# The state space scan of a hybrid encoder: rotation, scan and turn back worked in place in PSUM

## The chip, the cores and the metric

The kernel runs on one core of a Trainium2 chip. Its engines are named as the profile names them: PE (matrix products, with PEld for its weight loads), DVE (vector), ACT (scalar), POOL, and SP, which only issues DMAs here. The metric is the device time of one execution, in microseconds (us), the median over runs. Each engine has its own in-order queue of instructions; an instruction may first wait for semaphores that other engines, or earlier instructions, raise.

## The reference

A trunk of two layers on 256 tokens of width 1024. Layer 0 mixes tokens by a bidirectional diagonal complex state space (S5), layer 1 by dilated window attention; each layer then attends to 256 memory tokens and ends in a squared-ReLU MLP. Only the state space part is touched by the change:

```python
def s5_direction(u, lam_re, lam_im, log_dt, b_re, b_im, c_re, c_im, reverse):
    """u: (B,S,G,16) float32 -> Re(C x_t): (B,S,G,16)."""
    ...
    abar_re = mag * jnp.cos(ang)
    abar_im = mag * jnp.sin(ang)
    ...
    bu_re = jnp.einsum('bsgc,gpc->bsgp', u, bbar_re)
    bu_im = jnp.einsum('bsgc,gpc->bsgp', u, bbar_im)
    ...
    _, _, xr, xi = lax.associative_scan(combine, (a_re, a_im, bu_re, bu_im),
                                        reverse=reverse, axis=1)
    return jnp.einsum('bsgp,gcp->bsgc', xr, c_re) - jnp.einsum('bsgp,gcp->bsgc', xi, c_im)
```

There are 64 groups of 16 channels, 64 complex states per group and two directions. The state follows x(t) = A x(t-1) + B u(t) with a complex diagonal A; the result goes through a gelu and a gated product (GLU).

## The kernel before

**What stands where.** The state space part runs first, then the products that make keys and values of the memory tokens, then GLU, memory attention and MLP of layer 0, then layer 1. The memory's keys and values need nothing from the state space part, so their float32 products (`gemm32`, line 241) are mixed into PE's queue between the state space products, as fill. A framework's scheduler, which works with its own estimates, puts the instructions of the whole program into each engine's queue in advance; program order gives the priorities. On the chip that order is fixed.

**The state space part** (`s5`) works through eight chunks of eight groups each (here a chunk is always such a set of groups; tokens are taken four at a time, which gives 64 positions). A tile of a chunk is 128 rows (direction and state) by 8 groups x 64 positions = 512 numbers, which in float32 is just one PSUM bank. The steps per chunk:

- input weights (`s5_weigh_in`, lines 1029 to 1031): six products and sums on DVE, all operands in SBUF, give V; PE transposes V (line 1036) and ACT copies it from PSUM to VT (line 1038).
- `turn` (lines 749 to 752 on POOL): six products and sums make the rotation table T, two tiles (real, imaginary); T exists twice, so the table of a chunk waits until the scan two chunks earlier has read its own.
- `drive` (line 1075): 32 small products on PE put the chunk's inputs, real and imaginary, into two PSUM banks.
- `scan` (below), on DVE: rotates the inputs into a frame in which A is real (complex product with T), runs a linear recurrence along the positions (`tensor_tensor_scan`, line 1093, with the magnitudes R, which ACT writes at lines 1085 and 1086), and turns the result back (complex product with conjugate T, lines 1097 to 1099). ACT then copies the result xt into X (lines 1102 and 1103).
- `weigh_out` on POOL (lines 1113 to 1115): six products and sums, the output weights W; they are kept for three chunks.
- `impulse` (lines 1130 and 1135): products on PE for the response within four tokens, through DRAM into a small matrix M.
- `read` (lines 1156, 1158): PE reads the states out with X, W and M; gelu on ACT, four transposes on PE (line 1164), a copy on ACT (line 1167), a subtraction on DVE (line 1168), which makes the input of GLU.

The loop calls, for each chunk `ch`: the input weights, turn and drive of `ch + 1`, the scan of `ch`, its impulse response, the read of `ch - 1` and the output weights of `ch + 1`. The scheduler runs the input weights one chunk further ahead, so DVE's queue alternates: scan of `ch`, input weights of `ch + 2`, scan of `ch + 1`.

**PSUM** has eight banks. In this part three hold sums of the memory products and five (`psb`) serve all the rest in turn: transposes of the input weights (two per chunk), the drive's two banks, impulse (one), read and its transposes (two). Before the change a drive's two banks are last read by the fifth DVE instruction of the scan; everything behind works in SBUF tiles: `tmp` (two buffers), z and xt.

## Time and profile before

| What | Value |
| --- | --- |
| Median of 3 runs | 1143.39 us (1140.92 to 1145.66) |
| The profiled execution, its span | 1146.1 us |
| Busy PE / DVE / ACT / POOL, whole span | 1055.5 / 761.0 / 576.5 / 240.5 us |
| Mean granted PE clock | 0.940 |
| State space loop (97.4 to 213.5 us): PE / DVE / POOL busy | 96.42 / 113.29 / 88.83 of 116.10 us, clock 0.76 |

The profile shows one execution; the page states no time for it but its span, from the first to the last instruction. Busy time is that of an engine's own instructions, so an engine that is busy all the time may still be held up inside an instruction, and one that is idle costs nothing unless others wait for it. Rows of the timeline give the start, the length and the instruction, in square brackets the idle time before it and what ended it; each float32 product of PE stands there as two records. Groups by line give shortest, median and longest length in ns.

### The profile page before, as it was taken

How to read it: one execution, taken by the hardware profiler on the slowest of the kernel's cores; microseconds unless marked ns; L12 is line 12 of the kernel's file. 1: busy time of each engine (PE TensorE's matmuls, PEld its weight loads, DVE VectorE, ACT ScalarE, POOL GpSimd, SP SyncE). 2: the span in 40 equal slices, each digit the busy share in tenths (PEclk: the TensorE clock that was granted, in tenths of full speed). 3: DMA queues.
4: the chain of work that ended last, by engine and by line, in shares of the span. 5: the costliest groups of instructions: out<-in, count | busy, mean ns of one | idle time of the engine just before them, and what ended most of it. 6: DMA issues, size and time to landing. Idle time of an engine off the chain costs nothing. (4 is left out here: it accounts for less than half of the span.)

```text
span 1146.1 us, 16845 instructions
## 1 busy us (share of the span) xinstructions
PE 1055.5 (92%) x6526; PEld 866.0 (76%) x6526; DVE 761.0 (66%) x1103; ACT 576.5 (50%) x1024; POOL 240.5 (21%) x186
## 2 busy tenths in 40 slices
PE   4787789899999966999998999999999999999998
PEld 3444455556879856899986887887878988998997
DVE  7999999933768633544456676777864776545444
ACT  6253332336757534444444565576753655545443
POOL 3978877400200001100104003000010000111000
PEclk8788677699999987999998999999999999999999
DMA  8312112235554346565655555545433425555653
GB/s 176 93 50 78 62 32 65 70 100 169 187 170 140 116 101 143 189 199 189 189 180 183 168 175 159 177 154 168 148 113 107 155 103 166 184 186 181 196 190 111
DMA packets 99768, 164.02 MB, mean 143 GB/s; under 512 B 16701, under 2 KB 28551, under 8 KB 99560
## 3 DMA queue, kind: packets, MB, share of 16 engines
q1 hardware_dynamic: 88612, 157.15, 43.6%
q10 hardware_dynamic: 11076, 5.80, 2.7%
q8 instruction: 51, 0.84, 0.3%
q14 instruction: 29, 0.24, 0.1%
HBM read 159.11 MB, written 3.82 MB: 142 GB/s over the span
## 5 line engine op out<-in xcount | busy, mean ns | idle before, releaser
L155 DVE TENSOR_TENSOR wlo<-raw,whi 128x1024 fp32r<-128x1024 f32 x264 | 330.6, 1254 | 254.3 <-ACT whi L154 252.7
L154 ACT CAST whi<-raw 128x1024 fp32r<-128x1024 f32 x264 | 276.5, 1049 | 241.0 <-PE psa L202 137.3
L200 PE MATMUL psa<-whi,xs 128*128 128x512 f32 x448 | 179.2, 400 | 0.7 <-ACT sg L1198 0.7
L201 PE MATMUL psa<-wlo,xs 128*128 128x512 f32 x448 | 178.2, 398 | 0.0
L202 PE MATMUL psa<-whi,xs 128*128 128x512 f32 x448 | 177.8, 397 | 0.0
L272 PE MATMUL psb<-xs,whi 128*128 128x256 f32 x512 | 146.1, 286 | 19.7 <-ACT whi L154 19.7
L285 POOL TENSOR_TENSOR sq<-rl 128x512 f32<-128x512 f32 x32 | 40.0, 1251 | 543.6 <-ACT rl L284 543.6
L276 PE MATMUL psb<-xs,wlo 128*128 128x256 f32 x512 | 145.6, 285 | 0.8 <-DVE wlo L155 0.8
L274 PE MATMUL psb<-xs,whi 128*128 128x256 f32 x512 | 145.6, 285 | 0.0
L272 PEld LDWEIGHTS psb<-xs,whi 128*128 128x128 f32 x512 | 99.1, 194 | 20.8 <-ACT whi L154 19.9
L241 PE MATMUL psa<-raw,mT 128*128 128x512 f32 x192 | 103.9, 690 | 0.3 <-DMA raw<-in_xattn_w_kv 0.3
L201 PE MATMUL psa<-wlo,hh 128*128 128x512 f32 x256 | 99.8, 390 | 0.0
L200 PE MATMUL psa<-whi,hh 128*128 128x512 f32 x256 | 99.8, 390 | 0.0
L202 PE MATMUL psa<-whi,hl 128*128 128x512 f32 x256 | 99.7, 389 | 0.0
L276 PEld LDWEIGHTS psb<-xs,wlo 128*128 128x128 f32 x512 | 98.9, 193 | 1.0 <-DVE wlo L155 1.0
L274 PEld LDWEIGHTS psb<-xs,whi 128*128 128x128 f32 x512 | 99.1, 193 | 0.5
L200 PEld LDWEIGHTS psa<-whi,xs 128*128 128x128 f32 x448 | 85.2, 190 | 17.4 <-ACT sg L1198 1.2
L202 PEld LDWEIGHTS psa<-whi,xs 128*128 128x128 f32 x448 | 85.2, 190 | 16.7
L201 PEld LDWEIGHTS psa<-wlo,xs 128*128 128x128 f32 x448 | 85.1, 190 | 16.7 <-DVE wlo L155 0.9
L241 PEld LDWEIGHTS psa<-raw,mT 128*128 128x128 f32 x192 | 40.6, 224 | 43.4 <-issue 41.6
L202 PEld LDWEIGHTS psa<-whi,hl 128*128 128x128 f32 x256 | 48.1, 188 | 10.0
L200 PEld LDWEIGHTS psa<-whi,hh 128*128 128x128 f32 x256 | 48.1, 188 | 9.7
(326 smaller groups left out, 1703.0 us busy)
## 6 DMA issues: line engine op xcount, KB each, us to landing
raw<-in_mlp_w SPq DMA_DIRECT2D x128, 512.0 KB, 3.9
raw<-in_attn_w_qkv SPq DMA_DIRECT2D x72, 512.0 KB, 3.7
raw<-in_xattn_w_kv SPq DMA_DIRECT2D x32, 512.0 KB, 4.1
raw<-in_s_w_glu SPq DMA_DIRECT2D x16, 512.0 KB, 3.8
raw<-in_xattn_w_q SPq DMA_DIRECT2D x16, 512.0 KB, 3.4
raw<-in_xattn_w_o SPq DMA_DIRECT2D x16, 512.0 KB, 4.0
raw<-in_attn_w_o SPq DMA_DIRECT2D x8, 512.0 KB, 3.4
bias_d<-f ACTq DMA_DIRECT2D x1, 1536.0 KB
```

Of the source, the lines that this page charges most:

```text
L154: self.nc.scalar.copy(hi, src)
L155: self.nc.vector.tensor_sub(lo, src, hi.bitcast(F32))
L200: nc.tensor.matmul(acc[t], xh[:, k0 + k, sl], hi[:, k % 2, :], start=st, stop=False)
L201: nc.tensor.matmul(acc[t], xh[:, k0 + k, sl], lo[:, k % 2, :], start=False, stop=False)
L202: nc.tensor.matmul(acc[t], xl[:, k0 + k, sl], hi[:, k % 2, :], start=False, stop=en)
L241: nc.tensor.matmul(acc[t], xT[:, k + q, t * P:(t + 1) * P], raw[:, q, :], start=k + q == 0, stop=k + q == KT - 1)
L272: nc.tensor.matmul(o, hi[:, k % 2, fs], xh[:, kt, :], start=st, stop=False, skip_group_check=True)
L274: nc.tensor.matmul(o, hi[:, k % 2, fs], xl[:, kt, :], start=False, stop=False, skip_group_check=True)
L276: nc.tensor.matmul(o, lo[:, k % 2, fs], xh[:, kt, :], start=False, stop=en, skip_group_check=True)
L285: nc.gpsimd.tensor_mul(sq, rl, rl)
```

## The change

The complex products and the recurrence of `scan` no longer go through SBUF tiles. The two products with the real input go to two SBUF scratch tiles; the two with the imaginary input overwrite the two banks; sum and difference, the recurrence and, in the same order, the turn back work in place in the banks. Only the last sum and difference leave PSUM, into xt. The tile z is gone. Each DVE instruction of the scan has one input in PSUM and one in SBUF. The arithmetic is the same, with the same number of instructions. All other hunks remove only comments, and move line numbers behind the scan by 8.

```diff
         def scan(ch):
...
             nc.scalar.mul(R[:, :, 0:1], R[:, :, 0:1], 0.0)
-            z = ph.tile([P, 2, 8, 64], F32, tag="z", name="z")
             tm = lambda: self.tmp(early, 8, 64)
-            self.cmul(v, [z[:, 0], z[:, 1]], Ss.pop(ch), [T[:, 0], T[:, 1]], tm)
+            S0, S1 = Ss.pop(ch)
+            p, q = tm(), tm()
+            v.tensor_tensor(p, S0, T[:, 0], op=ALU.mult)
+            v.tensor_tensor(q, S0, T[:, 1], op=ALU.mult)
+            v.tensor_tensor(S0, S1, T[:, 1], op=ALU.mult)
+            v.tensor_tensor(S1, S1, T[:, 0], op=ALU.mult)
+            v.tensor_tensor(S0, p, S0, op=ALU.subtract)
+            v.tensor_tensor(S1, S1, q, op=ALU.add)
             rf = R.rearrange("p g k -> p (g k)")
-            for ri in range(2):
-                zf = z[:, ri].rearrange("p g k -> p (g k)")
+            for z in (S0, S1):
+                zf = z.rearrange("p g k -> p (g k)")
                 v.tensor_tensor_scan(zf, rf, zf, 0.0, op0=ALU.mult, op1=ALU.add)
             xt = ph.tile([P, 2, 8, 64], F32, tag="xt", name="xt")
-            for o, (p0, p1, op) in enumerate(((0, 1, ALU.add), (1, 0, ALU.subtract))):
-                t0, t1 = tm(), tm()
-                v.tensor_tensor(t0, T[:, p0], z[:, 0], op=ALU.mult)
-                v.tensor_tensor(t1, T[:, p1], z[:, 1], op=ALU.mult)
-                v.tensor_tensor(xt[:, o], t0, t1, op=op)
+            p, q = tm(), tm()
+            v.tensor_tensor(p, S0, T[:, 0], op=ALU.mult)
+            v.tensor_tensor(q, S0, T[:, 1], op=ALU.mult)
+            v.tensor_tensor(S0, S1, T[:, 1], op=ALU.mult)
+            v.tensor_tensor(S1, S1, T[:, 0], op=ALU.mult)
+            v.tensor_tensor(xt[:, 0], p, S0, op=ALU.add)
+            v.tensor_tensor(xt[:, 1], q, S1, op=ALU.subtract)
```

Since the scheduler orders the whole program, the built order is shown at two places (buffer numbers kept; SCALAR_TENSOR_TENSOR in these rows is the recurrence). First DVE, from the first instruction of the scan of chunk 2 to the first product of the turn back; `psb_897` and `psb_898` are the two banks, `xs_660` the rotation table. Before:

```order
L749 TENSOR_TENSOR tmp_1110<-psb_898,xs_660 128x512
L751 TENSOR_TENSOR tmp_1112<-psb_897,xs_660 128x512
L752 TENSOR_TENSOR z_1109<-tmp_1112,tmp_1110 128x512
L749 TENSOR_TENSOR tmp_1115<-psb_897,xs_660 128x512
L751 TENSOR_TENSOR tmp_1117<-psb_898,xs_660 128x512
L1093 SCALAR_TENSOR_TENSOR z_1109<-R_1106,z_1109 128x512
L752 TENSOR_TENSOR z_1109<-tmp_1117,tmp_1115 128x512
L1093 SCALAR_TENSOR_TENSOR z_1109<-R_1106,z_1109 128x512
L1097 TENSOR_TENSOR tmp_1123<-xs_660,z_1109 128x512
```

And with the change, where `psb_892` and `psb_893` are the banks:

```order
L1090 TENSOR_TENSOR tmp_1099<-psb_892,xs_660 128x512
L1091 TENSOR_TENSOR tmp_1100<-psb_892,xs_660 128x512
L1092 TENSOR_TENSOR psb_892<-psb_893,xs_660 128x512
L1093 TENSOR_TENSOR psb_893<-psb_893,xs_660 128x512
L1094 TENSOR_TENSOR psb_892<-tmp_1099,psb_892 128x512
L1095 TENSOR_TENSOR psb_893<-psb_893,tmp_1100 128x512
L1099 SCALAR_TENSOR_TENSOR psb_892<-R_1096,psb_892 128x512
L1099 SCALAR_TENSOR_TENSOR psb_893<-R_1096,psb_893 128x512
L1102 TENSOR_TENSOR tmp_1110<-psb_892,xs_660 128x512
```

The first recurrence stood before the second sum and now stands behind it; the place of the scan between the input weights on DVE's queue is the same.

Second PE, from the transposes of the last input weights (`V`) to the drive of the last chunk (L1075), with the semaphores that a row waits for. Before:

```order
L1036 MATMUL psb_1783<-ident_67,V_1771 128x128 [waits DVE_49]
L1036 MATMUL psb_1783<-ident_67,V_1771 128x128 x3
L1036 MATMUL psb_1789<-ident_67,V_1771 128x128 [waits DVE_49]
L1036 MATMUL psb_1789<-ident_67,V_1771 128x128 x3
L241 MATMUL psa_2172<-raw_2173,mT_625 128x512
L241 MATMUL psa_2172<-raw_2179,mT_625 128x512 x2
L241 MATMUL psa_2171<-raw_2185,mT_625 128x512 [waits DMAHW4_49]
L241 MATMUL psa_2172<-raw_2185,mT_625 128x512
L241 MATMUL psa_2171<-raw_2185,mT_625 128x512
L1075 MATMUL psb_1805<-u2_487,VT_1782 64x64 [waits Activation_49]
```

And with the change:

```order
L1036 MATMUL psb_1753<-ident_67,V_1741 128x128 [waits DVE_49,PE_49]
L1036 MATMUL psb_1753<-ident_67,V_1741 128x128 x3
L241 MATMUL psa_2132<-raw_2133,mT_625 128x512
L241 MATMUL psa_2132<-raw_2139,mT_625 128x512 x2
L241 MATMUL psa_2131<-raw_2145,mT_625 128x512 [waits DMAHW4_49]
L1036 MATMUL psb_1759<-ident_67,V_1741 128x128 [waits DVE_49]
L1036 MATMUL psb_1759<-ident_67,V_1741 128x128 x3
L241 MATMUL psa_2132<-raw_2145,mT_625 128x512
L241 MATMUL psa_2131<-raw_2145,mT_625 128x512
L1075 MATMUL psb_1775<-u2_487,VT_1752 64x64 [waits DVE_49,Activation_49]
```

The second half of the transposes moved behind four fill products. Followed back to the instruction that raises the semaphore, both halves waited before for the first instructions of the scan of chunk 6 (L749, L751 reading its banks); now the second half waits for that scan's last sum (L1106), and the drive for its last difference (L1107). The same holds for the drives of chunks 4, 5 and 6 and the scan before each. Nearer the start, ten of the eleven fill products between the read of chunk 0 and its transposes stay there and one moves ahead of the read, which now waits for the last sum of the scan of chunk 1 to free its bank. POOL's and SP's order is the same, and so is every engine's behind the state space part.

## The prediction

> **What bounds the kernel now.** I read the page first: its 40 slices say which engine is full where.

> ```profile
> span 1146.1 us, 16845 instructions
> ...
> PE   4787789899999966999998999999999999999998
> ...
> DVE  7999999933768633544456676777864776545444
> ...
> POOL 3978877400200001100104003000010000111000
> PEclk8788677699999987999998999999999999999999
> ```

> A slice is 28.65 us. DVE stands at 9 from the second slice to the eighth, about 29 to 229 us; POOL is busy in the same stretch and nearly nowhere else, and the granted PE clock is low there (6 to 8 tenths). From the ninth slice on it is PE that stands mostly at 9. So the change, which touches the state space part alone, lies in the one stretch where DVE is full. Next the busy time by stretch, cut where each chunk's scan begins (columns: stretch, length, busy PE, PEld, DVE, ACT, POOL, granted clock, DMA share, GB/s).

> ```profile
> 97.40:121.10 23.70, 23.70 (x186) 14.05 (x186) 23.04 (x20) 9.82 (x16) 19.81 (x14) 0.90 0.23 63
> ...
> 191.20:213.50 22.30, 17.66 (x153) 10.78 (x153) 21.75 (x22) 8.69 (x16) 15.53 (x10) 0.73 0.21 63
> 213.50:233.70 20.20, 20.20 (x161) 12.78 (x162) 14.05 (x15) 4.57 (x7) 6.64 (x4) 0.64 0.30 91
> 233.70:270.50 36.80, 36.80 (x235) 21.66 (x233) 12.98 (x20) 12.20 (x21) 0.00 (x0) 1.00 0.27 80
> 270.50:360.00 89.50, 87.62 (x459) 73.31 (x458) 61.54 (x86) 66.89 (x132) 8.47 (x4) 1.00 0.57 184
> ...
> 97.40:213.50 116.10, 96.42 (x845) 60.41 (x846) 113.29 (x105) 41.50 (x75) 88.83 (x59) 0.76 0.19 56
> ```

> In the loop (97.4 to 213.5) DVE is busy 113.29 of 116.10 us, PE 96.42, at a clock of 0.76. From 213.5 PE takes over: it has no idle time up to 270.5, and almost none after. So DVE sets the pace to the end of scan 6 (the scan of chunk 6; chunks count from 0), PE after it, and a gain counts only if it brings PE earlier to the point where PE is never idle again. Now the same DVE instructions by line (shortest/median/longest ns).

> ```profile
> L749 DVE TENSOR_TENSOR tmp<-psb,xs x15: 690/691/693, 69.0 to 233.7; 128x512 f32<-128x512 f32 x15
> L751 DVE TENSOR_TENSOR tmp<-psb,xs x15: 678/680/681, 69.6 to 234.3; 128x512 f32<-128x512 f32 x15
> L752 DVE TENSOR_TENSOR z<-tmp x14: 666/1514/1707, 70.3 to 217.9; 128x512 f32<-128x512 f32 x14
> L1093 DVE TENSOR_TENSOR_SCAN z<-R,z x14: 1214/1990/2151, 73.1 to 218.6; 128x512 f32<-128x512 f32 x14
> L1097 DVE TENSOR_TENSOR tmp<-xs,z x14: 660/1086/1687, 78.6 to 224.4; 128x512 f32<-128x512 f32 x14
> L1098 DVE TENSOR_TENSOR tmp<-xs,z x14: 677/684/1748, 80.0 to 226.0; 128x512 f32<-128x512 f32 x14
> L1099 DVE TENSOR_TENSOR xt<-tmp x14: 691/692/1667, 81.8 to 226.7; 128x512 f32<-128x512 f32 x14
> L1029 DVE TENSOR_TENSOR tmp<-tav,bb x13: 691/1665/1687, 65.4 to 210.6; 128x512 f32<-128x512 f32 x13
> L1168 DVE TENSOR_TENSOR xs<-psb,xs x5: 409/411/417, 133.9 to 227.3; 128x256 fp32r<-128x256 f32 x5
> ```

> This is the view that decides. All products and sums but L1168 have 128x512 elements. The two lines that read one PSUM bank and one SBUF tile (L749, L751) take 690 to 693 and 678 to 681 ns every time, with POOL beside them or not. Each line that reads two SBUF tiles has the same shortest time, 660 to 692, and a longest of 1667 to 1748. So something makes a DVE instruction with two SBUF inputs wait, and one with one SBUF input not; POOL, busy 88.83 of 116.10 us (the last row of the fence above), reads SBUF all that time.

> **The change, part by part.** The count stays: 12 products and sums and 2 scans per chunk. What goes is the second SBUF input of ten of the 14. What it costs today, from the timeline (start, length, instruction):

> ```profile
> 69.01 0.69 DVE L749 TENSOR_TENSOR tmp<-psb,xs 128x512 f32<-128x512 f32 x1 [0.35 <-PE psb L1075]
> 69.62 0.68 DVE L751 TENSOR_TENSOR tmp<-psb,xs 128x512 f32<-128x512 f32 x1
> 70.33 1.54 DVE L752 TENSOR_TENSOR z<-tmp 128x512 f32<-128x512 f32 x1
> ...
> 87.99 1.48 DVE L1029 TENSOR_TENSOR tmp<-tav,bb 128x512 f32<-128x512 f32 x1
> ...
> 97.44 0.69 DVE L749 TENSOR_TENSOR tmp<-psb,xs 128x512 f32<-128x512 f32 x1
> ...
> 111.69 1.68 DVE L1029 TENSOR_TENSOR tmp<-tav,bb 128x512 f32<-128x512 f32 x1
> ...
> 121.10 0.69 DVE L749 TENSOR_TENSOR tmp<-psb,xs 128x512 f32<-128x512 f32 x1
> ...
> 213.48 0.69 DVE L749 TENSOR_TENSOR tmp<-psb,xs 128x512 f32<-128x512 f32 x1
> ...
> 219.70 1.69 DVE L1097 TENSOR_TENSOR tmp<-xs,z 128x512 f32<-128x512 f32 x1
> ...
> 249.10 0.67 DVE L1097 TENSOR_TENSOR tmp<-xs,z 128x512 f32<-128x512 f32 x1
> ...
> 252.46 0.69 DVE L1099 TENSOR_TENSOR xt<-tmp 128x512 f32<-128x512 f32 x1
> ```

> Scan 0 lasts from 69.01 to 87.99, 19.0 us. Scan 1 lasts 14.25 (97.44 to 111.69), the input weights of a later chunk behind it (six products and sums, L1029 to L1031, all with two SBUF inputs, not touched) 9.4 (to 121.10), and this pair is typical: five such periods (97.44 to 213.48) take 116.0, 23.2 each. Undisturbed, today's form takes 10.3: its first half 213.48 to 219.70, 6.2, and its second half 249.10 to 252.46+0.69, 4.05, both beside an idle or waiting POOL.

> New form. An instruction that needs nothing from the one before starts 0.61 after it (69.01 to 69.62), one that needs its result 0.71 (69.62 to 70.33). Today five of the products and sums follow at the longer step, in the new order two (the new L1092 and L1104, which wait until the product before them has read the bank): -0.3. Eight instructions now write PSUM from DVE, and no row shows such a write. Lower bound of its cost: nothing, as for a read (L749 at 691 against 691 to 692 for L1099 undisturbed); a gain is excluded, since no product here takes under 660. Upper bound, the nearest longer row: that of an instruction that waits for POOL, 1514, 0.82 more. I take 0.05 each, next to the reads, since reading the same bank costs 0 to 0.03: +0.4. The scan itself takes 1214 undisturbed at 512 elements, over twice the time per element of a product, so its arithmetic sets its rate and I leave it at 1.21. A scan of the chunk is then 10.3 again, now beside a busy POOL.

> [...]

> DVE's sum to the end of scan 6: scan 0 19.0 - 10.3 = 8.7; scans 1 to 5, 5 x (14.25 - 10.3) = 19.8; scan 6 starts at 213.48 and takes 13.9 today (until the evacuation at 227.33, below): 3.6. Together 32.1. The input weights gain nothing: they meet POOL instruction for instruction already (L1029 median 1665), and will again, because POOL's table for a later chunk waits until the scan lets go of the buffer (18.9 us in five waits, next fence) and so starts when the weights do. POOL itself is no bound: 88.83 us busy over five periods is 17.8 each, its waits for DVE included in the instructions' lengths, under the new period of 23.2 - 3.95 = 19.3.

> ```profile
> 227.33 0.42 DVE L1168 TENSOR_TENSOR xs<-psb,xs 128x256 fp32r<-128x256 f32 x1
> ...
> 106.88 0.45 PE L1156 MATMUL psb<-W,xs 128*64 128x64 f32 x4
> ...
> 137.33 0.69 PE L1156 MATMUL psb<-W,xs 128*64 128x64 f32 x4
> ...
> 158.72 0.45 PE L1156 MATMUL psb<-W,xs 128*64 128x64 f32 x4
> ...
> 210.79 0.66 PE L1156 MATMUL psb<-W,xs 128*64 128x64 f32 x4 [4.64 <-DVE xs L1168]
> ...
> 232.40 1.16 PE L1075 MATMUL psb<-u,VT 64*64 64x64 f32 x64
> 233.50 0.45 PE L1156 MATMUL psb<-W,xs 128*64 128x64 f32 x4
> ...
> POOL xs L752 <- DVE tmp L1098: 18.9, 5, 4.5
> ...
> PE psb L1075 <- ACT VT L1038: 7.1, 2, 5.6
> ```

> The banks are the price. A pair of banks with a chunk's inputs was free for PE after the first five DVE instructions of its scan (L751); now it is held to the last (new L1106, L1107). Five banks serve this whole part in turn, so from chunk 4 on PE's drive of a chunk stands behind the end of the scan before it, where it stood behind the fifth instruction; behind the drive on PE's queue stand the impulse response, the read of the chunk before and the fill products of L241. The release comes 10.3 - 3.3 = 7 us later in its scan than now (3.3 being the first five undisturbed). In that time PE has its fill, so I cost it at nothing while PE is the later one, and at 7 us of idle a chunk where PE has none left; today it idles there for ACT's copies of VT (7.1 us in two waits).

> PE's own account: its read 0 started at 106.88 and waits in the new build for a bank until the end of scan 1, 97.44 - 8.7 + 10.3 = 99.0; with some 0.4 to start behind it that is still 7.5 earlier than today. From read 0 to read 5 (233.50) it takes 126.6 today, 25.3 a chunk, waits included. Two of these rounds had next to no wait: 137.33 to 158.72, 21.4, and 210.79 to 233.50, 22.7. Five rounds at 21.4 to 22.7 save 13.1 to 19.6. So PE reaches read 5, and with it the last drive (232.40), 20.6 to 27.1 earlier; DVE alone would allow 32.1. PE is the later one; I take **25**, in the upper part because waits that fall away raise the clock (0.64 to 0.90 in the loop, 1.00 in the full stretch behind it). From there PE's 36.8 us up to 270.5 are full and unchanged, the order behind is the same on every engine, and DVE has 12.98 of 36.80 to do there: the gain reaches the end. The profiled execution's 1146.1 becomes 1121; it lies 2.7 above the median of the runs, 1143.4, so the median becomes **1118**.

> **The rivals.** *The held banks keep PE idle (0.16).* PE's 19.7 us of idle in the loop (116.10 - 96.42) stay almost whole, moved to the ends of scans, and only the 7.5 at read 0 and some 4 of the rest come through: 1131. For it: PE already waits on these banks today, and a wait lowers its clock. Against: DVE's period falls to 19.3, below PE's best round, so PE should rarely arrive first. [...]

> *Reading and writing one bank takes turns (0.09).* From 256 to 512 elements a product grows from 411 to 691, 1.09 ns per element; if a write to PSUM took that once more, each of eight writers would be 0.56 longer, 4.5 a scan, 31.5 over seven: the whole 32.1 is eaten. No change, 1143. Nothing in the trace shows the case; the reads at full rate speak against it a little.

> *Slower (0.06).* The write also holds up the dependent instruction behind it until it is through, and each writer costs the 0.82 of the upper bound: 6.6 a scan, 46 over seven, 14 more than is saved: 1157. It decides from 32.1 / 56 = 0.57 per writer.

> *PE keeps its full clock (0.04).* Then its 96.42 busy us at 0.76 shrink to about 73, DVE is the bound, and its 32 come through: 1111. Against: PE then waits for DVE, and waits have cost it the clock.

> That the change does nothing, POOL delaying the new forms too, is excluded for one PSUM and one SBUF input by L749 and L751 (15 each, 3 ns apart). No row shows a scan in that form. [...]

> **How the numbers follow.** Forecast 0.65, rivals 0.16, 0.09, 0.06, 0.04. A measurement of this kernel tells a change from none at about 0.5%, 5.7 us. Faster: 0.65 + 0.16 + 0.04 = 0.85; same 0.09; slower 0.06. The range from 1109 (DVE's whole 32.1, and 2 for the spread of the runs) to 1136 (the 7.5 of read 0 alone) leaves out the two rivals without a gain and little else.

> **What would show it.** Right: every product and sum of the scan under 0.75 us and the scans near 1.21 with POOL beside them; DVE's period at 19 to 20; L1029 of the weights still above 1.6; PE's last drive at 205 to 212; no difference in what follows. Wrong: a same-bank instruction (new L1093, L1095, L1105) above 1.2 while new L1090 stays at 0.69 shows the bank taking turns; PE idle over 15 us in the loop, ended by new L1106 or L1107, shows the held banks; products above 1.3 on lines with one SBUF input show that POOL was not the cause. If L1029 to L1031 take under 5 us together, I have misread whom POOL meets, and the gain is larger.

## The result and the profile after

The changed kernel takes 1105.36 us (median of 4 runs, 1104.76 to 1107.67), the kernel before 1144.53 (1140.92 to 1147.14): a ratio of 0.9664, 95% interval 0.9641 to 0.9687. That is 39 us, or 3.4%, where 25 were forecast (1118, range 1109 to 1136); the time lies below the range. The page of the profiled execution (a slice is now 27.6 us):

```profile
span 1104.0 us, 16864 instructions
...
PE   4789799999999849999999999999999999999998
DVE  7999998337687425554467777687945766545444
PEclk8789988999999969999999999999999999999999
```

DVE is still at 9 from the second slice, but only to the sixth, and PEclk, which stood at 6 to 8 tenths in the second to the eighth slice, is at 7 to 9 there now. DVE's instructions by line (shortest/median/longest ns):

```profile
L1090 DVE TENSOR_TENSOR tmp<-psb,xs x8: 692/692/692, 67.8 to 195.7; 128x512 f32<-128x512 f32 x8
L1092 DVE TENSOR_TENSOR psb<-psb,xs x8: 699/700/700, 69.2 to 197.1; 128x512 f32<-128x512 f32 x8
L1093 DVE TENSOR_TENSOR psb<-psb,xs x8: 689/690/690, 69.8 to 197.7; 128x512 f32<-128x512 f32 x8
L1095 DVE TENSOR_TENSOR psb<-psb,tmp x8: 693/693/693, 71.0 to 198.9; 128x512 f32<-128x512 f32 x8
L1099 DVE TENSOR_TENSOR_SCAN psb<-R,psb x16: 1202/1211/1229, 71.6 to 210.0; 128x512 f32<-128x512 f32 x16
L1106 DVE TENSOR_TENSOR xt<-tmp,psb x8: 677/678/679, 76.4 to 213.6; 128x512 f32<-128x512 f32 x8
L1029 DVE TENSOR_TENSOR tmp<-tav,bb x14: 677/1492/1670, 62.2 to 176.6; 128x512 f32<-128x512 f32 x14
L1031 DVE TENSOR_TENSOR V<-tmp x14: 691/1370/1640, 63.5 to 179.8; 128x512 f32<-128x512 f32 x14
```

Every line with one PSUM and one SBUF input has nearly the same length all the time, the recurrence too (1.21 us; a median of 1.99 before). L1093 reads and writes one bank and takes 690 ns, against 692 of L1090, which writes to SBUF, and the longest line that writes a bank takes 700 (L1092): the write costs next to nothing. L1029 and L1031 of the input weights, with two SBUF inputs, still reach 1.6 us and more. The timeline of DVE:

```profile
67.83 0.69 DVE L1090 TENSOR_TENSOR tmp<-psb,xs 128x512 f32<-128x512 f32 x1 [0.27 <-PE psb L1075]
...
77.57 1.59 DVE L1029 TENSOR_TENSOR tmp<-tav,bb 128x512 f32<-128x512 f32 x1
...
87.14 0.69 DVE L1090 TENSOR_TENSOR tmp<-psb,xs 128x512 f32<-128x512 f32 x1
...
180.64 0.69 DVE L1090 TENSOR_TENSOR tmp<-psb,xs 128x512 f32<-128x512 f32 x1
...
190.38 0.42 DVE L1176 TENSOR_TENSOR xs<-psb,xs 128x256 fp32r<-128x256 f32 x1
```

A scan takes 9.74 us (67.83 to 77.57), a period 18.7 (87.14 to 180.64, five of them), and scan 6 ends at 190.38 instead of 227.33. PE:

```profile
96.51 0.42 PE L1164 MATMUL psb<-W,xs 128*64 128x64 f32 x4 [0.76 <-DVE xt L1106]
...
115.16 1.16 PE L1075 MATMUL psb<-u,VT 64*64 64x64 f32 x64 [2.51 <-DVE xs L1176]
...
153.32 0.33 PE L1075 MATMUL psb<-u,VT 64*64 64x64 f32 x4 [2.07 <-DVE xt L1106]
...
157.81 0.69 PE L1164 MATMUL psb<-W,xs 128*64 128x64 f32 x4
...
194.43 1.16 PE L1075 MATMUL psb<-u,VT 64*64 64x64 f32 x64
195.52 0.45 PE L1164 MATMUL psb<-W,xs 128*64 128x64 f32 x4
```

Read 0 starts at 96.51 (before 106.88), the last drive at 194.43 (before 232.40), read 5 at 195.52 (before 233.50): 38.0 earlier. The stretches between read 0 and read 5, of before and of the changed kernel (columns as in the prediction: stretch, length, busy PE, PEld, DVE, ACT, POOL, each with its count of records, granted clock, DMA share, GB/s):

```profile
106.88:233.50 126.62, 106.94 (x888) 67.00 (x887) 118.00 (x111) 43.52 (x78) 86.23 (x57) 0.74 0.21 62
```
```profile
96.51:195.52 99.01, 91.03 (x884) 57.26 (x884) 91.81 (x106) 41.64 (x73) 77.25 (x59) 0.91 0.25 78
```

Of the 27.6 us that these five rounds are shorter, 11.7 are PE's idle time (19.68 to 7.98) and **15.9 are PE's busy time** (106.94 to 91.03) for practically the same products (888 and 884 records), at a clock of 0.91 instead of 0.74. PE as a whole is best compared from the start of scan 0 to PE's first GLU product (the first of L200 that reads the state space part's result), since it has practically the same products there, 1463 to 1466 records, in every kernel of the table below:

```profile
69.01:294.20 225.19, 193.66 (x1463) 121.80 (x1464) 182.14 (x176) 92.60 (x179) 126.64 (x85) 0.82 0.26 80
```
```profile
67.83:256.30 188.47, 175.17 (x1466) 110.69 (x1465) 146.44 (x176) 92.68 (x179) 108.61 (x85) 0.94 0.30 95
```

225.19 = 193.66 busy + 31.53 idle before; 188.47 = 175.17 + 13.30 after. Of the 36.7 gained, 18.2 is idle time and 18.5 busy time. POOL gains too: its same 85 instructions take 108.6 us in this stretch instead of 126.6. GLU starts 37.9 earlier. The 4 us by which the two spans differ beyond that lie far behind, in parts that the change does not touch, where the granted clock of this one execution of before was a little lower (0.97 against 1.00 from 554 to 652 us of before); between the medians there are 39.2.

### The profile page after: what moved, and what is told of

Same layout as the page of the kernel before. It is cut to its first block, busy times and chain, and to the rows that moved or that the text cites. A ratio compares the mean times of both kernels' runs of the same rounds, so it can differ in the third digit from the quotient of the medians.

```text
span 1104.0 us, 16864 instructions
## 1 busy us (share of the span) xinstructions
PE 1031.8 (93%) x6526; PEld 851.0 (77%) x6526; DVE 725.4 (66%) x1103; ACT 576.5 (52%) x1024; POOL 222.2 (20%) x186
## 5 line engine op out<-in xcount | busy, mean ns | idle before, releaser
L200 PE MATMUL psa<-whi,xs 128*128 128x512 f32 x448 | 177.7, 397 | 0.7 <-ACT sg L1206 0.7
L202 PE MATMUL psa<-whi,xs 128*128 128x512 f32 x448 | 176.6, 394 | 0.0
L200 PE MATMUL psa<-whi,hh 128*128 128x512 f32 x256 | 99.8, 390 | 0.0
L200 PEld LDWEIGHTS psa<-whi,xs 128*128 128x128 f32 x448 | 84.2, 188 | 17.1 <-ACT sg L1206 1.2
L201 PEld LDWEIGHTS psa<-wlo,xs 128*128 128x128 f32 x448 | 84.3, 188 | 16.6 <-DVE wlo L155 0.8
L241 PE MATMUL psa<-raw,mT 128*128 128x512 f32 x192 | 96.5, 647 | 0.0
L241 PEld LDWEIGHTS psa<-raw,mT 128*128 128x128 f32 x192 | 37.5, 207 | 38.5 <-issue 37.4
L200 PEld LDWEIGHTS psa<-whi,hh 128*128 128x128 f32 x256 | 48.1, 188 | 9.6
```

The source lines that it names most:

```text
L200: nc.tensor.matmul(acc[t], xh[:, k0 + k, sl], hi[:, k % 2, :], start=st, stop=False)
L201: nc.tensor.matmul(acc[t], xh[:, k0 + k, sl], lo[:, k % 2, :], start=False, stop=False)
L202: nc.tensor.matmul(acc[t], xl[:, k0 + k, sl], hi[:, k % 2, :], start=False, stop=en)
L241: nc.tensor.matmul(acc[t], xT[:, k + q, t * P:(t + 1) * P], raw[:, q, :], start=k + q == 0, stop=k + q == KT - 1)
```

## The experiments

In each the figure to compare beside the time is this account of PE, from scan 0 to the first GLU product. The last column is the mean of the five periods from the start of scan 1 to that of scan 6:

| Kernel | Median us | Stretch | PE busy | PE idle | Clock | DVE period |
| --- | --- | --- | --- | --- | --- | --- |
| before | 1144.5 | 225.2 | 193.7 | 31.5 | 0.82 | 23.2 |
| results to SBUF | 1149.3 | 230.1 | 191.0 | 39.1 | 0.84 | 23.4 |
| changed | 1105.4 | 188.5 | 175.2 | 13.3 | 0.94 | 18.7 |
| two more products | 1107.6 | 189.6 | 175.8 | 13.8 | 0.94 | 19.7 |
| turn back to SBUF | 1113.4 | 193.8 | 177.5 | 16.3 | 0.93 | 19.9 |
| changed, without POOL | 1088.9 | 171.9 | 167.9 | 4.0 | 0.98 | 16.0 |
| before, without POOL | 1087.1 | 172.6 | 167.5 | 5.1 | 0.98 | 15.7 |
| table in PSUM, four banks | 1092.6 | 170.3 | 166.1 | 4.2 | 0.99 | 15.5 |

**Is it the second SBUF input?** First the new sequence with the old kind of operands:

```diff
-            v.tensor_tensor(S0, S1, T[:, 1], op=ALU.mult)
-            v.tensor_tensor(S1, S1, T[:, 0], op=ALU.mult)
+            z = ph.tile([P, 2, 8, 64], F32, tag="z", name="z")
+            v.tensor_tensor(z[:, 0], S1, T[:, 1], op=ALU.mult)
+            v.tensor_tensor(z[:, 1], S1, T[:, 0], op=ALU.mult)
+            S0, S1 = z[:, 0], z[:, 1]
```

> The scan keeps the new sequence of products and sums, but everything behind the two banks goes back to an SBUF tile (z), so ten of its 14 instructions read two SBUF tiles again. Theory (the second SBUF input was the cost): these ten take 0.8 or more longer beside POOL, a scan again takes 13.5 to 15 us, and the time goes back to 1136 to 1148. Rival (the gain came from the sequence, which puts fewer dependent instructions behind each other): scans near 10.3 and 1104 to 1110.

Measured 1149.28 (1146.92 to 1153.10, 10 runs), 1.0041 of the kernel before (1.0023 to 1.0058): the whole gain is gone, and a little more. By line:

```profile
L1104 DVE TENSOR_TENSOR tmp<-z,xs x7: 660/1524/1700, 75.8 to 217.3; 128x512 f32<-128x512 f32 x7
L1101 DVE TENSOR_TENSOR_SCAN z<-R,z x14: 1194/2054/2282, 71.6 to 216.2; 128x512 f32<-128x512 f32 x14
L1109 DVE TENSOR_TENSOR xt<-tmp,z x7: 678/1748/1764, 83.5 to 224.2; 128x512 f32<-128x512 f32 x7
```

The recurrence is back at a median of 2.05 us, the sum into xt at 1.75. (The banks come free earlier here, so the scheduler also sends a few first products of the next scan ahead; that did not help.) The sequence is not what gains, and PE's account, 191.0 busy and 39.1 idle, is close to that of before again (193.7 and 31.5).

Then POOL's work in the loop was left out of both kernels; all scans then use the first chunk's table and all reads its output weights:

```diff
             if ch < 7:
                 self.s5_weigh_in(early, ch + 1)
-                turn(ch + 1)
                 drive(ch + 1)
...
             if ch < 7:
-                weigh_out(ch + 1)
+                Ws[ch + 1] = Ws[0]
```

> The changed kernel without POOL's work in the loop: rotation table and output weights are made for chunk 0 only and used for all chunks (so the result is not the reference's); everything else stays. Theory (what is left of the disturbance is the input weights against POOL, and PE is faster than 20 us a round if it is not kept waiting): weights 4.2 instead of 8.7, DVE period near 14, PE becomes the bound with rounds of 16 to 17.5 and a clock of 1.0, and the time 1085 to 1095. Rival, as predicted (PE cannot go below 20 a round): 1099 to 1106.

> The kernel before with the same piece left out (POOL's rotation tables and output weights for chunks 1 to 7). Theory (two SBUF inputs cost nothing unless POOL reads SBUF beside them): every line of the scan at 0.66 to 0.70, the recurrence at 1.21, a scan near 10.3, and the time within 4 us of the changed kernel without POOL, so the change is worth nothing there. Rival (the PSUM forms are faster by themselves, or the sequence is): the scans stay 3 us or more longer than the changed kernel's, and the time 10 us or more above it.

Measured 1088.93 (1085.77 to 1089.75; ratio to before 0.9505, 0.9476 to 0.9534) and 1087.14 (1086.16 to 1090.90; 0.9500, 0.9470 to 0.9531): without POOL's work the change is worth nothing in time. First the kernel before without POOL, DVE's lines and then its timeline over one scan:

```profile
L1097 DVE TENSOR_TENSOR tmp<-xs,z x16: 664/678/694, 73.2 to 194.4; 128x512 f32<-128x512 f32 x16
L1099 DVE TENSOR_TENSOR xt<-tmp x16: 680/691/693, 74.5 to 195.8; 128x512 f32<-128x512 f32 x16
L1029 DVE TENSOR_TENSOR tmp<-tav,bb x12: 682/692/694, 77.3 to 156.1; 128x512 f32<-128x512 f32 x12
```
```profile
81.53 0.69 DVE L749 TENSOR_TENSOR tmp<-psb,xs 128x512 f32<-128x512 f32 x1
...
91.90 0.69 DVE L1029 TENSOR_TENSOR tmp<-tav,bb 128x512 f32<-128x512 f32 x1
```

Then the timeline of the changed kernel without POOL over one scan, and its stretches from scan 1 to scan 6 and from scan 0 to GLU (columns as above):

```profile
78.58 0.69 DVE L1090 TENSOR_TENSOR tmp<-psb,xs 128x512 f32<-128x512 f32 x1
...
88.31 0.69 DVE L1029 TENSOR_TENSOR tmp<-tav,bb 128x512 f32<-128x512 f32 x1
```
```profile
78.58:158.76 80.18, 80.18 (x810) 48.49 (x812) 69.10 (x104) 39.05 (x70) 0.00 (x0) 1.00 0.30 93
64.61:236.50 171.89, 167.88 (x1463) 105.81 (x1464) 119.25 (x176) 91.98 (x178) 8.93 (x8) 0.98 0.31 98
```

The lines with two SBUF tiles do not pass 0.70 any more, in any chunk. An undisturbed scan takes 10.37 in the old form (81.53 to 91.90) and 9.73 in the new (78.58 to 88.31): 0.64 less, with fewer instructions that wait for the one just before them, and nothing to be seen of the writes (L1093, which writes a bank, takes 690 ns here too). The recurrence in its new form, which the prediction found in no row, is not lengthened beside POOL either: L1099 of the changed kernel takes 1.20 to 1.23 us with POOL at work, and as much without (1201 to 1229 ns). And PE, whose queue has the same order as in the changed kernel, needs 167.88 us for its products here, not 175 or 194, and idles 4.0. From scan 1 to scan 6 it is busy without a gap, at a clock of 1.00, while DVE works 69.10 of 80.18 us: here PE is the bound, at 16.0 us a round. So its floor for the stretch is near 172, 16.6 below the changed kernel, and a round of 20 us was not its limit.

**DVE or PE?** The same stretch, from scan 1 to scan 6, of the changed kernel:

```profile
87.14:180.64 93.50, 84.76 (x836) 52.81 (x834) 91.02 (x104) 39.13 (x71) 81.58 (x63) 0.91 0.24 75
```

DVE is busy 91.02 of 93.50 us and waits once, for 0.5 us; PE idles 8.7 us, and all its waits there end with a DVE instruction. In the next two runs DVE gets more work. First the turn back gets its SBUF tiles back:

```diff
-            p, q = tm(), tm()
-            v.tensor_tensor(p, S0, T[:, 0], op=ALU.mult)
-            v.tensor_tensor(q, S0, T[:, 1], op=ALU.mult)
-            v.tensor_tensor(S0, S1, T[:, 1], op=ALU.mult)
...
+            for o, (p0, p1, op) in enumerate(((0, 1, ALU.add), (1, 0, ALU.subtract))):
+                t0, t1 = tm(), tm()
+                v.tensor_tensor(t0, T[:, p0], S0, op=ALU.mult)
+                v.tensor_tensor(t1, T[:, p1], S1, op=ALU.mult)
+                v.tensor_tensor(xt[:, o], t0, t1, op=op)
```

> The changed kernel with the turn back's two products with the imaginary part written to SBUF tiles, as in the kernel before, so that two of its 14 instructions (the sum and the difference into xt) read two SBUF tiles again. These two take 0.5 to 0.9 longer each, 1 to 1.8 us more DVE per scan. If DVE sets the pace, 7 to 12 later: 1113 to 1117. If PE is the later one, as the runs with more and with less DVE work say: 0 to 3 later, 1105 to 1109.

Measured 1113.38 (1109.65 to 1115.69), 8 over the changed kernel. The row of its sums by line, and PE's longest wait (us in total, times, longest):

```profile
L1105 DVE TENSOR_TENSOR xt<-tmp x16: 691/693/1672, 74.3 to 218.9; 128x512 f32<-128x512 f32 x16
```
```profile
PE psb L1075 <- DVE tmp L1103: 6.4, 2, 4.6
```

Fewer than half of the sums are lengthened (a median of 0.69, up to 1.67). The fill products, transposes and drives stand in PE's queue as in the changed kernel. DVE's period is 1.2 longer, 6.2 over five, and the stretch of PE 5.3 longer: nearly one for one. So in the changed kernel it is **DVE that sets the pace** in the loop, and the expectation that PE is the later one falls. The second experiment:

```diff
             p, q = tm(), tm()
             v.tensor_tensor(p, S0, T[:, 0], op=ALU.mult)
+            for _ in range(2):
+                v.tensor_tensor(p, S0, T[:, 0], op=ALU.mult)
```

> The changed kernel with the first product of each scan issued two more times (same operands, same result): 2 x 0.69 = 1.4 us more of DVE per scan, none of it contended. Theory (DVE sets the pace from scan 0 to scan 6, PE has slack in the loop): 7 x 1.4 = 9.7 later, 1113 to 1117. Rival, as predicted (PE is the later one, its rounds are what lasts): PE's rounds of 20 us against a DVE period of 18.7 + 1.4 = 20.1 leave 0 to 2 of it, 1104 to 1108.

Measured 1107.64 (1106.40 to 1109.88), 2.3 over the changed kernel. The period grew to 19.7, 5 us over five, but the stretch by 1.1. Taken alone this speaks for the other side. But the scheduler had also put more fill products into these rounds (12 ahead of a chunk's transposes where there were 10, 8 between transposes and drive where there were 7): from scan 1 to scan 6 PE works off 897 records here, 836 in the changed kernel, and so has less left behind the loop. And none of the reads runs at half clock (8 of 64 rows do in the changed kernel). So it is no clean test of DVE; how much of the difference to the run above is due to either was not tried by itself.

**What the waits do to the clock.** In finer stretches the granted clock of these profiles has two values, 1.00 and 0.50. Two stretches of before (the first holds read 4, in the second of the prediction's two rounds), then one of the changed kernel:

```profile
210.79:226.12 15.33, 15.33 (x98) 11.14 (x99) 14.99 (x16) 3.47 (x8) 7.32 (x5) 0.50 0.28 86
...
228.30:232.40 4.10, 4.10 (x10) 1.52 (x8) 0.00 (x0) 1.24 (x2) 0.00 (x0) 1.00 0.72 202
```
```profile
155.50:171.50 16.00, 16.00 (x93) 11.27 (x85) 15.55 (x19) 6.00 (x13) 11.34 (x9) 0.50 0.07 17
```

In the first PE was busy all 15.33 us, at half clock throughout; the clock had gone down within the 4.64 us of waiting ahead of it and came back only 2 us into a run of full-width fill products (L241, from 226.12). In the changed kernel it went down twice, for 6.8 us from 73.1 on, and at 155.0, 1.7 us behind the end of a wait of 2.07 us (at 153.32, quoted above), for 17.1 us, through read 3 at 0.69 a row instead of 0.45. To see whether the clock is what lengthens PE's own work, with POOL and DVE as before:

```diff
             ps = self.psb()
+            for _ in range(4):
+                nc.tensor.matmul(ps, self.ident, self.bb[:, 0, 0:32, :].rearrange("p a c -> p (a c)"), start=True, stop=True)
             for j in range(8):
```

> The kernel before with four extra PE products of 128x512 ahead of each chunk's read, into the bank that the read then overwrites: 8 x 2.4 us of PE at full clock. In the kernel before the reads of chunks 1, 3 and 4 ran in part or whole at half the clock (0.69 us for a row of four products instead of 0.45), without any idle time inside them, after a wait ahead of them. Theory (a wait puts the clock to one half, small products do not bring it back, a run of full-width products does within 2 to 3 us): nearly all reads at 0.45, the clock between scan 0 and GLU from 0.82 to 0.88 or more, and the time 5 to 20 later than before, less than the 25 that 32 such products take at 0.6 to 1.0 us. Rival (POOL's or DVE's load sets the clock): the same share of reads at half clock, clock 0.78 to 0.84, 20 to 30 later.

Measured 1164.45 (1161.05 to 1165.49), ratio 1.0163 (1.0135 to 1.0191). PE's groups by line, the reads and the extra products (count | busy, mean ns | idle), then its account:

```profile
L1158 PE MATMUL psb<-W,xs 128*64 128x64 f32 x256 | 28.5, 234 | 0.0
L1154 PE MATMUL psb<-bb,ident 128*128 128x512 f32 x64 | 34.0, 681 | 0.0
```
```profile
67.35:314.10 246.75, 210.58 (x1534) 126.41 (x1535) 188.00 (x179) 94.03 (x182) 131.92 (x86) 0.90 0.23 74
```

All 64 rows of the reads are at 0.45 (before, 21 of 64 were at 0.66 or 0.69). Without the 34.0 us of extra products PE is busy 176.6 us, 17 less than in the kernel before, although it idles 36.2, 5 more. So in these runs half clock set in within or behind a wait (of 4.64 and 2.07 us above) and ended in a run of full-width products, and it was not an effect of POOL's or DVE's load (131.92 and 188.00 us busy here, 126.64 and 182.14 before). Half of the 34.0 us (19 to 25 had been reckoned) came back through it; with longer waits ahead of the drives 20.3 remain, 0.3 over the most that was expected.

**The banks.** One more for the state space part, one fewer for the memory products:

```diff
-            with k.banks(3, 5):
+            with k.banks(2, 6):
```

> The changed kernel with six PSUM banks for the state space part and two (instead of three) for the sums of the memory products. In the changed kernel PE idles 5 us in all for banks that a scan still holds (waits ended by L1106 and L1107). Theory (holding the banks costs little): these waits go and the time falls by 0 to 5, 1100 to 1106, unless the memory products now wait for one of their two banks, which would give some of it back (up to 1112). Rival (the held banks are what keeps PE from more): 1090 to 1098.

Measured 1112.91 (1110.44 to 1115.87), 7.5 slower than the changed kernel. PE's wait for a bank that a scan holds (us, times, longest), of the changed kernel and of this one, and the account of this one:

```profile
PE psb L1075 <- DVE xt L1106: 4.3, 2, 2.3
```
```profile
PE psb L1075 <- DVE xt L1106: 2.7, 1, 2.7
```
```profile
68.33:265.50 197.17, 184.95 (x1478) 117.24 (x1479) 150.83 (x183) 94.29 (x182) 112.31 (x84) 0.90 0.29 93
```

The wait at the drive falls from 4.3 us to 2.7, and PE idles 12.2 instead of 13.3, but its busy time rises by 10, of which 1.7 are 12 transposes of a later part that stand ahead of GLU only here: 20 of the reads' 64 rows run at 0.69, 8 in the changed kernel. PE now waits 3.1 us ahead of a read. Neither the theory nor the rival came about, and since the memory products lost a bank, this run does not decide on the held banks; the last one below does.

**The weights.** Their six instructions still read two SBUF tiles. Three edits, alone and together: the second product to a PSUM bank (sum from PSUM), the factor table in a bank of its own, taken from the memory products (table in PSUM) or from the five (table, four banks):

```diff
-            t0, t1 = self.tmp(early, 8, 4, 16), self.tmp(early, 8, 4, 16)
+            t0, t1 = self.tmp(early, 8, 4, 16), self.psb().rearrange("p (g s c) -> p g s c", g=8, s=4)
```
```diff
-        self.tav = table("tav", rows(av))
+        tv = self.ptv.tile([P, 8, G], F32, name="tavp")
+        for q, x in enumerate(rows(av)):
+            nc.tensor.transpose(tv[:, q], flat(x), self.ident[:G, :G])
+        self.tav = tv
...
-            with k.banks(3, 5):
+            with k.banks(2, 5), tc.tile_pool(name="ptv", bufs=1, space=PSUM) as k.ptv:
```

In the run with four banks the last line has `k.banks(3, 4)`.

> The changed kernel, and of the input weights' six instructions the second product goes to a PSUM bank instead of an SBUF tile, so that the sum (L1031) reads one SBUF tile. Theory (the second SBUF input is the cost): L1031 falls from a median of 1.4 to 0.69, 1.4 to 1.7 us less DVE per chunk. By the run without POOL (4.5 us less per chunk gave 16 us) this is worth 4 to 6: 1099 to 1102. Rival (the two further banks per chunk, of five, make PE or DVE wait): 1106 to 1115.

> The changed kernel, and the table of the input weights' factors (tav, 512 numbers a partition) stays in a PSUM bank of its own, taken from the memory products (two banks instead of three), so that the four products L1029 and L1030 read one SBUF tile. Theory: L1029 and L1030 fall from 1.4 to 1.6 to 0.69, 3 to 3.5 us less DVE per chunk; three quarters of the 16 us without POOL, 1092 to 1097. Rival (with two banks the memory products wait for their copies, and PE is what sets the end): 1100 to 1112.

> Both: the table in a PSUM bank and the second product in a bank of the five. No instruction of scan or weights reads two SBUF tiles. Theory: the DVE period of the run without POOL (14 us) with POOL at work, 1086 to 1093. Rival (the banks now keep engines waiting): 1096 to 1112.

> As the run with the table of the input weights in a PSUM bank of its own, but the bank is taken from the state space part (four instead of five) and the memory products keep three. There the DVE period fell to 15 us and the gain was lost behind the loop, where PE waited for ACT's copies of the memory products' two banks and then ran at half clock. Theory (that loss came from the two banks): with three of them it goes, and the time is 1092 to 1099. Rival (four banks are too few when a scan holds two to its end): PE and DVE wait for banks inside the loop, 1104 to 1115.

The sum from PSUM: 1118.56 (1116.14 to 1120.35), 13 slower than the changed kernel and beyond its rival's range too, though L1031 does what was expected of it. Its row, and DVE's greatest wait (us, times, longest):

```profile
L1031 DVE TENSOR_TENSOR V<-tmp,psb x14: 670/678/687, 66.1 to 200.1; 128x512 f32<-128x512 f32 x14
```
```profile
DVE xs L1176 <- ACT xs L1175: 38.1, 6, 7.6
```

Each chunk now takes two more of five banks, and DVE's queue stands six times for the copy behind a read that PE has not come to; the period is 24.4 from chunk 1 to chunk 5. Both together: 1115.75 (1114.98 to 1116.77), with the same wait at 55.7 us in seven, where 1086 to 1093 was expected. The table alone, with two banks for the memory products: 1103.00 (1102.75 to 1106.95; 0.9642, 0.9620 to 0.9664), not to be told from the changed kernel: the theory failed and the rival's time came. DVE's period there is 15.6, yet behind scan 7's start (171.03) PE has waits for ACT, of 0.7 and 0.9 us at 178 and of 2.6 ahead of L200 for a copy of the memory products (0.9 in the changed kernel), and 7 rows of the reads run at half clock. That stretch:

```profile
171.00:190.00 19.00, 17.42 (x137) 13.08 (x138) 10.20 (x15) 6.35 (x14) 0.00 (x0) 0.67 0.13 39
```

With the bank taken from the five instead: **1092.55** (1089.37 to 1093.56), ratio to before 0.9536 (0.9513 to 0.9558), 13 us faster than the changed kernel. Its four products of the weights by line, and the account of PE:

```profile
L1032 DVE TENSOR_TENSOR tmp<-tavp,bb x13: 680/691/692, 61.2 to 158.1; 128x512 f32<-128x512 f32 x13
L1033 DVE TENSOR_TENSOR tmp<-tavp,bb x14: 672/680/682, 59.7 to 158.7; 128x512 f32<-128x512 f32 x14
```
```profile
68.71:239.00 170.29, 166.05 (x1464) 104.93 (x1462) 126.22 (x176) 91.27 (x177) 102.06 (x84) 0.99 0.34 105
```

POOL works 102 us in that stretch, PE needs 170.3, as without POOL (171.9), at a clock of 0.99, and all 64 rows of the reads are at 0.45. The rival, four banks too few, did not come about; with one bank fewer and two still held through each scan PE idles 4.2 us, so the held banks are not what keeps PE from more. This pair of times speaks for the memory products' two banks as what cost the run before its gain; by which wait they did it is not shown.

## Why the prediction was wrong, and what of it was right

- **The cause was right.** The second SBUF input beside POOL is the whole gain: with it back, 1149.3; without POOL, the two kernels take 1088.9 and 1087.1.
- **The cost of the scan was a little too high.** "Eight instructions now write PSUM ... I take 0.05 each": they cost next to nothing (686 to 700 against 673 to 692 of the products that write to SBUF). The new order, taken at -0.3, saves 0.64. 10.3 became 9.74, the period 18.7 instead of 19.3. From the start of scan 0, scan 6 ends 35.8 earlier (158.3 before, 122.6 after), where 32.1 was worked out. An undisturbed product takes 691 ns with a PSUM input (L749 before) and 691 without (L1099 of the kernel before without POOL). One reading was off without weight in the sum: a recurrence of 1.21 us is 1.8 times a product of 0.69, not over twice; that its arithmetic sets its rate was the author's estimate, which no run shows.
- **The weights were right:** 8.4 to 9.6 us after, 9.4 before, L1029 still at a median of 1.49 (1.6 was named), POOL's table again beside them.
- **The step that failed is PE's own account, and with it "PE is the later one":** "Two of these rounds had next to no wait ... Five rounds at 21.4 to 22.7 save 13.1 to 19.6." They took 99.0, 19.8 each, and saved 27.6. The two rounds that served as PE's best had indeed little idle time, but they were not at full clock: the second stood at 0.50 for its first 15.3 us, and read 1 ran at 0.69 a row. The prediction's own rows show it: reads 1 and 4 begin with 0.69 and 0.66, reads 0, 2 and 5 with 0.45. So these two rounds, without waits of their own, were not rounds at full speed. At a clock of 1.00 a round took 16.0 (the changed kernel without POOL), less than DVE's 18.7. With next to no wait PE's floor for the stretch is near 172, 16.6 under what DVE allows, so DVE stays the bound and its whole gain comes through. The clock was given as a reason for "the upper part", without a number; the busy time that fell with it is 15.9 of the 27.6. With read 0 10.4 earlier instead of 7.5 (1.2 of that is the earlier scan 0, 1.1 the two shorter scans) PE reaches read 5 38.0 earlier, not 20.6 to 27.1 (the last drive at 194.4, where 205 to 212 was named).
- **The rival "PE keeps its full clock" (0.04)** has the right bound: DVE's whole gain comes through, 32 by its sum (1111), 36 as measured, and the time is 1105. Its way there was not what happened: the clock rose to 0.91 in the five rounds, not to 1.00, and PE's busy time fell from 106.9 to 91.0, less than in proportion to the clock, by which the rival had reckoned. The objection to it, that PE would go on waiting for DVE, was wrong in amount: PE idles 13.3 instead of 31.5.
- **The held banks (0.16)** cost 5.3 us of idle time (waits ended by L1106 and L1107, of 13.3) and did not keep the gain away. **Taking turns** in a bank (L1093 reads and writes one: 690 ns) and the **slower** case did not occur.
- **The tail** was right: the 87.5 us behind PE's full stretch (270.5 to 358 before, 232.5 to 320 after) have PE busy 85.62 in both.

## What to carry to other kernels

Where DVE and POOL work side by side, look at the spread of a line: the same instruction at 0.69 and 1.7 us, and the lines with one SBUF input without spread, meant here that where the operands lie was worth more than the count of instructions; one input, or an in-place result, in PSUM took the spread away: the recurrence beside POOL took 1.21 us instead of 1.99, and POOL's same 85 instructions 108.6 instead of 126.6. Before taking a stretch of PE as its floor, read the granted clock of that very stretch. Where a bank taken for DVE's sake comes from has to be tried: the same edit gave 2 us, within the noise, or 13, depending on the pool it was taken from.

## What the runs showed that was not expected

```profile
110.63:114.05 3.42, 2.02 (x13) 1.13 (x10) 3.39 (x6) 2.08 (x5) 3.26 (x4) 1.00 0.09 29
114.05:117.46 3.41, 2.30 (x97) 2.06 (x98) 3.41 (x6) 1.21 (x2) 3.33 (x4) 1.00 0.40 147
...
151.59:155.01 3.42, 1.51 (x68) 1.34 (x72) 3.42 (x7) 1.19 (x2) 2.26 (x2) 1.00 0.51 166
```

The wait of 2.51 us that ends at 115.16 (quoted above) lies across a point: PE works 2.02 and 2.30 us in the stretches on either side, and the clock stays at 1.00 (it does from 87 to 144). The shorter wait of 2.07 us lies almost whole within one stretch, which leaves 1.51 us of work in it, and the clock falls at its end. Every fall in this part of the two kernels stands behind a stretch with at most 2.00 us of work (1.48, 0.00, 1.40, 2.00, 1.78 and 1.84 before, 1.57 and 1.51 in the changed kernel); one stretch with 1.45, all of it 128x512 products (131.11 to 134.53), kept the clock, so the kind of product seems to count, which was not tried by itself.

Once down, the clock stayed down through 15.33 us in the kernel before (from 210.79) and 16.00 in the changed one (from 155.50) in which the profile shows PE busy without a gap, mostly with small products (64 columns) and transposes; it came back behind stretches with 1.1 to 3.4 us of 128x512 products in them, but not behind two with 2.07 us of them (from 218.92 before and from 165.98 in the changed kernel), so how much it takes stays open. And a wait cost more here than its own length: from the kernel before to the changed one without POOL, 27 us less idle time (31.5 to 4.0) went with 26 less busy time for the same products. It is no fixed rate, since the run with results in SBUF idled 7.6 us more than the kernel before and was busy 2.7 less.
